# Two trunk layers in fp32: the first sum of weight blocks in the seven products, by an adding DMA load instead of VectorE

## The chip, the cores and the metric

The kernel runs on one core of a Trainium2 chip. The metric is the device time of one execution in microseconds (us). The engines are TensorE (PE, matmuls; PEld is its weight load), VectorE (DVE), ScalarE (ACT), GpSimd (POOL) and SyncE (SP), which here issues loads. Each engine works through its own list of instructions in order and waits on semaphores for others. DMA transfers are issued on an engine's queue and run on 16 DMA engines.

## The reference

Two layers run over 128 context tokens and 512 latent tokens, 640 in all, of width 1024. Each layer has two feed-forward parts (FFNs) with a mixer between them; the first layer's mixer is a convolution beside a gated recurrence, the second's is attention. All is float32. What the change touches is the first product of the four FFNs:

```python
def swiglu(h, w_in, w_out):
    gt, up = jnp.split(h @ w_in, 2, axis=-1)
    return (jax.nn.silu(gt) * up) @ w_out

def ffn_sublayer(x, mod, g, w_in, w_out, slot):
    h = pre_norm(x, g, mod[:, 3 * slot], mod[:, 3 * slot + 1])
    return x + 0.5 * mod[:, 3 * slot + 2] * swiglu(h, w_in, w_out)
```

`w_in` is 1024 x 5632 (2816 gate columns, then 2816 up columns), `w_out` 2816 x 1024.

## The kernel before

**Precision.** A float32 matmul is made of three matmuls of parts: each operand is split into a high part, rounded by a cast on ScalarE (line 609), and a low part, the rest, by a subtraction on VectorE (line 610). `split_x` makes both.

**The first product of an FFN.** The 2816 gate and up columns are cut into 22 blocks of 128 columns; block j has a gate block and an up block of 1024 x 128 each. The first two blocks are multiplied plainly (`plain_pair`). The other 20 go through `strassen`, a scheme with seven products in the place of eight: the weights are the 2 x 2 blocks a11, a12 (first and second half of the rows of the gate block), a21, a22 (of the up block), each 512 x 128; the tokens are halves of 320. Every product is 12 matmuls of 128 x 320 (four row tiles, three terms). Four products need sums of weight blocks, made on VectorE by `summed` (line 742):

```python
S1 = a21 + a22    # product 5
S2 = S1 - a11     # product 6
S3 = a11 - a21    # product 7
S4 = a12 - S2     # product 3
```

and products 1, 2 and 4 take a11, a12 and a22 as they are. The weights of product i of block j, cast and low part, lie in a tile `ws{i}_{j}`. Over four FFNs this makes 80 blocks and 80 sums of each kind. The results are put together by VectorE (lines 780, 784, 788) and ScalarE (lines 778, 786) and written as high and low parts of the hidden activations, `g{j}`.

**Order.** `ffn` writes a list of jobs (block, product). Within a block the order is 1, 5, 6, 2, 7, 3, 4; at the start of an FFN the first two blocks with seven products are mixed: (2,1), (2,2), (3,1), (3,2), then (2,5) and the rest. Blocks come in four parts of 6, 6, 6 and 4; after each part `project_out` multiplies by the rows of `w_out` (matmuls `po`, line 623) and frees `g`. Before the seven products the token sums are made by `norm_sums`: `t13_q` on VectorE (line 546), `t24_q` on GpSimd (lines 547, 548), and their high and low parts (`tchi`, `tclo`, `tdhi`, `tdlo`, two tiles of half the sum each).

**Loads.** `load_w` (line 567) loads a weight block on SyncE's queue into one of 4 `raw` buffers, at a raised priority (`AHEAD`, 400), so that a scheduler puts the load before other work of its time. A load whose buffer is not free stops SyncE's queue.

**Slots.** Sums and other passing tiles are put by `slot()` into 18 slots of 128 x 640 and into halves of pair tiles; `free()` gives them back, and a slot freed longest ago is taken first. A tile put in a used slot waits for the slot's last reader. S1 is freed after S2 is made, S2 and S4 after product 3's parts, S3 after product 7's. Some tiles print under an older name of their buffer (an S1 as `ma`, for one).

The names in the rows: `raw_wg`, `raw_wu` gate and up block, `S` any of the four sums, `ws` their parts, `pa`, `pb`, `pc` the PSUM banks of the products (product 5 opens `pc`), `st` results on their way, `po` the output projection.

Of the kernel before, what the change touches and what calls it, by code (L numbers as in the profile page):

```python
# [13 lines left out]
ALU = mybir.AluOpType  # L14
AX = mybir.AxisListType

P = 128
# [16 lines left out]
AHEAD = 400  # L34
# [41 lines left out]
def run(steps):  # L76
    for _ in steps:
        pass


class Trunk:
# [564 lines left out]
    def ffn(self, l, which, n, last):  # L646


        w_out = self.i["ffn_w_out"][l, which]
        pairs = {}  # L650
        mm = self.bank["mm"]
        ring = {"b": mm[0:3], "c": mm[3:5], "a": mm[5:6]}
        g = {}

        def bank(kind, name):
            ring[kind].append(ring[kind].pop(0))
            return self.psum.tile([P, 512], F32, tag=f"bank{ring[kind][-1]}", name=name)[:, 0:HW]

        def do(j, i):
            p = pairs.setdefault(j, dict(done=set()))  # L660
            for r, nm in enumerate(("gate", "up")):
                if nm not in p and (r == 0 or i not in (1, 2)):
                    p[nm] = self.load_w(*self.ffn_first(l, which, j)[r])
            self.strassen(p, j, i, bank, g)

        plain = EARLY if n == 0 else PLAIN
        order = [(j, c) for j in range(plain) for c in range(2)]
        if n:
            order.sort(key=lambda x: x[1])
        weights = {}  # L670
        for j, c in order:
            if j not in weights:
                weights[j] = [(self.weights(*x), x[1]) for x in self.ffn_first(l, which, j)]
            self.plain_pair(j, c, weights[j], g)
        self.free(*[f"b12_{q}" for q in range(4)])
        for q in range(4):
            self.norm_sums(q)
        jobs, ends = [], {}
        for part, (f0, fn) in enumerate(PARTS):
            js = list(range(f0, f0 + fn))  # L680
            if part == 0:
                js = js[plain:]
                first = js[:FIRST_TWO]
                jobs += [(j, i) for j in first for i in (1, 2)]
                jobs += [(first[0], i) for i in (5, 6, 3, 7)]
                for j, nxt in zip(first, first[1:]):
                    jobs += [(nxt, 5), (j, 4), (nxt, 6), (nxt, 3), (nxt, 7)]
                nxt = js[FIRST_TWO]
                jobs += [(nxt, 1), (first[-1], 4)] + [(nxt, i) for i in (5, 6, 2, 7, 3, 4)]
                js = js[FIRST_TWO + 1:]  # L690
            jobs += [(j, i) for j in js for i in (1, 5, 6, 2, 7, 3, 4)]
            ends[len(jobs)] = part
        self.points = self.points[plain:]
        for at, (j, i) in enumerate(jobs):
            do(j, i)
            if i == 4:
                self.point()
                if (l, which, j) in self.pieces:
                    self.mod_piece(*self.pieces.pop((l, which, j)))
                    if not self.pieces:  # L700
                        self.free("cond32")
            if at + 1 in ends:
                part = ends[at + 1]
                f0, fn = PARTS[part]
                if part == len(PARTS) - 1:
                    self.free_operand()
                js = range(f0, f0 + fn)
                run(self.project_out(w_out[f0 * P:(f0 + fn) * P, :], [g[j][0] for j in js], [g[j][1] for j in js], n,
                                     final=(part == len(PARTS) - 1), last=last))
                self.free(*[f"g{j}" for j in js])  # L710
        if not last:
            self.norm_chunk(n + 1, 1)
# [19 lines left out]
    def strassen(self, p, j, i, bank, g):  # L732


        nc = self.nc
        a11, a12 = p["gate"][:, 0:4], p["gate"][:, 4:8]
        if "up" in p:
            a21, a22 = p["up"][:, 0:4], p["up"][:, 4:8]

        def summed(name, x, y, op):  # L740
            t = self.slot(f"{name}_{j}", n=512).rearrange("p (k m) -> p k m", m=P)
            nc.vector.tensor_tensor(out=t, in0=x, in1=y, op=op)  # L742
            p[name] = t
            return t

        with self.tc.high_priority(offset=SPLIT_AHEAD):
            if i == 5:
                src = summed("S1", a21, a22, ALU.add)
            elif i == 6:
                src = summed("S2", p["S1"], a11, ALU.subtract)  # L750
            elif i == 7:
                src = summed("S3", a11, a21, ALU.subtract)
            elif i == 3:
                src = summed("S4", a12, p["S2"], ALU.subtract)
            else:
                src = a11 if i == 1 else a12 if i == 2 else a22
            w = self.wp.tile([P, KD * P], F32R, tag="w", name=f"ws{i}_{j}").rearrange("p (k m) -> p k m", m=P)
            self.split_x(src, w[:, 0:4], w[:, 4:8])
            if i == 6:
                self.free(f"S1_{j}")  # L760
            elif i == 7:
                self.free(f"S3_{j}")
            elif i == 3:
                self.free(f"S2_{j}", f"S4_{j}")
        kind = {1: "b", 6: "b", 7: "b", 4: "b", 5: "c", 3: "c", 2: "a"}[i]
        if i in (1, 5, 2):
            p[kind] = bank(kind, f"p{kind}")
        ps = p[kind]
        x = {1: "11", 2: "21", 3: "22", 4: "T4", 5: "T1", 6: "T2", 7: "T3"}[i]
        for k in range(4):  # L770
            xhi, xlo = self.B[x, k]
            for t, (a, b) in enumerate(((w[:, k], xhi), (w[:, k], xlo), (w[:, 4 + k], xhi))):
                nc.tensor.matmul(ps, lhsT=a, rhs=b, start=(i in (1, 5, 2) and k == 0 and t == 0),  # L773
                                 stop=(k == 3 and t == 2), skip_group_check=True)
        with self.tc.high_priority(offset=POST_AHEAD):
            if i in (1, 5, 6):
                p[i] = t = self.stp.tile([P, HW], F32, tag="st", name=f"st{i}")
                nc.scalar.copy(out=t, in_=ps)
            elif i == 4:
                nc.vector.tensor_tensor(out=p[1], in0=p[1], in1=ps, op=ALU.mult)  # L780
                self.hidden(g, j, 0, p[1])
            else:
                t = p[{2: 1, 7: 5, 3: 6}[i]]
                nc.vector.tensor_tensor(out=t, in0=t, in1=ps, op=ALU.add)  # L784
                if i != 7:
                    nc.scalar.activation(out=t, in_=t, func=AF.Silu)
                if i == 3 and 7 in p["done"] or i == 7 and 3 in p["done"]:
                    nc.vector.tensor_tensor(out=p[6], in0=p[6], in1=p[5], op=ALU.mult)
                    self.hidden(g, j, 1, p[6])
        p["done"].add(i)  # L790
# [856 lines left out]
```

## Time and profile before

| | |
|---|---|
| time, median of 3 runs | 2524.88 us (2524.49 to 2527.0) |
| the profiled execution's own time | 2523.16 us |
| its span, first to last instruction | 2521.4 us |
| TensorE busy | 2437.3 us, 97% |
| VectorE busy | 1982.7 us, 79% |
| ScalarE busy | 1122.1 us, 45% |
| GpSimd busy | 224.5 us, 9% |
| mean granted TensorE clock | 0.989 |

The shares are means over the whole span; they tell which engine has no room, not where. The list of waits tells for what TensorE stood. The timeline tells at a place when an operation ended that gives a buffer back, and when the work that needs the next content began; the difference is what a later content may take. An operation on VectorE is longer in its row than the distance to the next start, since operations follow each other with an overlap.

### The profile page before, as it was taken

To read this page: it belongs to the slowest core of one execution; us is meant where nothing else is said; L and a number is where in the kernel's file an instruction comes from. 1 tells how busy PE (TensorE), PEld (TensorE's weight loads), DVE (VectorE), ACT (ScalarE), POOL (GpSimd) and SP (SyncE) were. 2 spreads that over 40 slices of the span, in tenths; PEclk is the share of its full clock that TensorE was granted. 3 is DMA by queue.
4 is the path that set the end of the run, shared out by engine and by line. 5 is a ranking of instruction groups with operands and counts; after the bars stand their busy time and mean duration, and the time that the engine had idled before them with its cause. 6 is when DMAs were issued, how large, how long until landed. Compare 5 with 4: busy or idle time off the path is not lost. (4 is left out here: it accounts for less than half of the span.)

```text
span 2521.4 us, 43474 instructions
## 1 busy us (share of the span) xinstructions
PE 2437.3 (97%) x17072; PEld 2347.9 (93%) x17072; DVE 1982.7 (79%) x3750; ACT 1122.1 (45%) x2278; POOL 224.5 (9%) x308
## 2 busy tenths in 40 slices
PE   7999999999989999999999999999999999999999
PEld 5889999998989989999999899999988899999999
DVE  6889888868997678988887788888777868585755
ACT  6425243543234452525255343434556655252533
POOL 0000000104234110000011000000132111000000
PEclk8999999999999999999999999999999999999999
DMA  8453534412111226343440644344300121232322
GB/s 246 123 178 115 150 113 142 142 46 60 55 45 39 78 67 184 107 137 105 138 139 24 193 122 133 112 129 126 100 28 15 35 80 44 75 87 82 89 80 76
DMA packets 378261, 254.53 MB, mean 101 GB/s; under 512 B 9302, under 2 KB 362953, under 8 KB 378057
## 3 DMA queue, kind: packets, MB, share of 16 engines
q1 hardware_dynamic: 373112, 248.35, 33.7%
q10 hardware_dynamic: 4944, 3.41, 0.5%
q8 instruction: 134, 2.20, 0.4%
q14 instruction: 71, 0.57, 0.1%
HBM read 248.32 MB, written 3.41 MB: 100 GB/s over the span
## 5 line engine op out<-in xcount | busy, mean ns | idle before, releaser
L623 PE MATMUL po<-g,whi_o 128*128 128x256 f32 (+2 forms) x2672 | 579.0, 309 | 2.7 <-DVE st L780 1.1
L623 PEld LDWEIGHTS po<-g,whi_o 128*128 128x128 f32 x2672 | 442.8, 188 | 12.3 <-issue 2.9
L623 PE MATMUL po<-g,wlo_o 128*128 128x256 f32 (+2 forms) x1336 | 408.5, 307 | 0.2 <-DVE wlo_o L610 0.2
L814 DVE SCALAR_TENSOR_TENSOR x<-po,modG,x 128x256 f32<-128x256 f32 (+3 forms) x480 | 196.5, 435 | 127.1 <-PE po L623 125.5
L349 DVE SCALAR_TENSOR_TENSOR ma<-raw_wm,cond,ma 128x512 f32<-128x512 f32 x364 | 263.7, 753 | 33.2 <-DMA raw_wm<-in_w_mod 33.0
L609 ACT CAST ws<-S 128x512 fp32r<-128x512 f32 x290 | 180.3, 622 | 222.0 <-DVE S L742 72.9
L609 ACT CAST whi_o<-raw_o 128x768 fp32r<-128x768 f32 (+1 forms) x142 | 110.4, 777 | 351.9 <-PE po L623 220.7
L623 PEld LDWEIGHTS po<-g,wlo_o 128*128 128x128 f32 x1336 | 250.8, 188 | 0.4 <-DVE wlo_o L610 0.4
L773 PE MATMUL pb<-tdhi,ws 128*128 128x320 f32 x960 | 222.9, 312 | 5.8 <-DVE st L784 4.9
L610 DVE TENSOR_TENSOR ws<-S,ws 128x512 fp32r<-128x512 f32 x290 | 199.1, 688 | 31.5 <-ACT ws L609 30.7
L773 PE MATMUL pc<-b,ws 128*128 128x320 f32 x1140 | 191.2, 309 | 0.0
L773 PE MATMUL pb<-tdlo,ws 128*128 128x320 f32 x600 | 184.9, 309 | 0.0
L773 PEld LDWEIGHTS pb<-tdhi,ws 128*128 128x128 f32 x960 | 162.2, 188 | 13.3 <-DVE st L784 9.6
L773 PEld LDWEIGHTS pc<-b,ws 128*128 128x128 f32 x1140 | 173.4, 188 | 0.0
L405 POOL TENSOR_TENSOR acc<-acc,sq 128x320 f32<-128x320 f32 (+2 forms) x38 | 37.6, 991 | 1351.4 <-ACT sq L404 955.5
L610 DVE TENSOR_TENSOR wlo_o<-raw_o,whi_o 128x768 fp32r<-128x768 f32 (+1 forms) x142 | 126.4, 890 | 30.8 <-ACT whi_o L609 18.9
L773 PE MATMUL pb<-b,ws 128*128 128x320 f32 x700 | 145.7, 309 | 0.8 <-DVE x L814 0.8
L609 ACT CAST ws<-raw_wg 128x512 fp32r<-128x512 f32 x160 | 98.9, 620 | 81.6 <-PE po L623 32.3
L610 DVE TENSOR_TENSOR ws<-raw_wg,ws 128x512 fp32r<-128x512 f32 x160 | 109.8, 688 | 27.8 <-ACT ws L609 27.7
L976 DVE SCALAR_TENSOR_TENSOR cw<-pad,vecs,cw 128x655 f32<-128x655 f32 x120 | 121.5, 1014 | 1.8
L773 PE MATMUL pb<-tclo,ws 128*128 128x320 f32 x400 | 122.2, 308 | 0.0
L773 PE MATMUL pa<-bchi,ws 128*128 128x320 f32 x520 | 116.2, 310 | 6.0 <-DVE st L784 6.0
(509 smaller groups left out, 5742.8 us busy)
## 6 DMA issues: line engine op xcount, KB each, us to landing
raw_wm<-in_w_mod SPq DMA_DIRECT2D x144, 512.0 KB, 4.0
raw_wg<-in_ffn_w_in SPq DMA_DIRECT2D x88, 512.0 KB, 4.1
raw_wu<-in_ffn_w_in SPq DMA_DIRECT2D x88, 512.0 KB, 4.0
raw_o<-in_ffn_w_out SPq DMA_DIRECT2D x96, 384.0 KB, 3.5
raw_o<-in_ffn_w_out SPq DMA_DIRECT2D x32, 256.0 KB, 3.0
raw_z<-in_ev_w_in SPq DMA_DIRECT2D x8, 512.0 KB, 3.9
raw_oq<-in_od_w_in SPq DMA_DIRECT2D x8, 512.0 KB, 5.0
raw_o<-in_od_w_out SPq DMA_DIRECT2D x16, 256.0 KB, 3.0
```

The costliest lines, as they stand in the source:

```text
L349: nc.vector.scalar_tensor_tensor(out=acc, in0=part, scalar=col, in1=acc, op0=ALU.mult, op1=ALU.add)
L405: nc.gpsimd.tensor_tensor(out=self.acc[:, c0:c0 + n], in0=self.acc[:, c0:c0 + n], in1=sq[:, 0:n], op=ALU.add)
L609: nc.scalar.copy(out=hi, in_=src)
L610: nc.vector.tensor_tensor(out=lo, in0=src, in1=hi.bitcast(F32), op=ALU.subtract)
L623: self.last_mm = nc.tensor.matmul(ps, lhsT=a[k], rhs=b[k][:, c0:c0 + n], start=(k == 0 and j == 0), stop=(k == nk - 1 and j == 2))
L773: nc.tensor.matmul(ps, lhsT=a, rhs=b, start=(i in (1, 5, 2) and k == 0 and t == 0), stop=(k == 3 and t == 2), skip_group_check=True)
L814: nc.vector.scalar_tensor_tensor(out=xs, in0=ps[:, s0 - c0:s0 - c0 + sn], scalar=self.modG[:, n, m, g:g + 1], in1=xs, op0=ALU.mult, op1=AL ...
L976: nc.vector.scalar_tensor_tensor(out=y, in0=x[:, j:j + T + 15], scalar=col(j), in1=y, op0=ALU.mult, op1=ALU.add)
```

## The change

The sum S1 is no longer made by VectorE. When `do` loads the up block of a block with seven products, it also takes the slot of S1 there, loads the first half of the up block's rows (a21) into it on SyncE's queue, and then adds the second half (a22) to it by a DMA on GpSimd's queue with `accum_op=add`. Each of the two moves 512 rows of 512 bytes, 256 KB. Both are at the raised priority `AHEAD`. `strassen` takes that tile as product 5's source. The whole up block is still loaded into its raw buffer for S3 and products 7 and 4. So 80 additions leave VectorE, and 80 loads on SyncE and 80 adding loads on GpSimd, which issued no DMA before, are new.

```diff
--- before.py
+++ after.py
@@ -661,6 +661,13 @@
             for r, nm in enumerate(("gate", "up")):
                 if nm not in p and (r == 0 or i not in (1, 2)):
                     p[nm] = self.load_w(*self.ffn_first(l, which, j)[r])
+                    if r:
+                        with self.tc.high_priority(offset=AHEAD):
+                            p["S1"] = self.slot(f"S1_{j}", n=512).rearrange("p (k m) -> p k m", m=P)
+                            up = self.ffn_first(l, which, j)[1][0]
+                            self.nc.sync.dma_start(out=p["S1"], in_=up[0:4 * P].rearrange("(k p) m -> p k m", p=P))
+                            self.nc.gpsimd.dma_start(out=p["S1"], in_=up[4 * P:].rearrange("(k p) m -> p k m", p=P),
+                                                     accum_op=ALU.add)
             self.strassen(p, j, i, bank, g)
 
         plain = EARLY if n == 0 else PLAIN
@@ -745,7 +752,7 @@
 
         with self.tc.high_priority(offset=SPLIT_AHEAD):
             if i == 5:
-                src = summed("S1", a21, a22, ALU.add)
+                src = p["S1"]
             elif i == 6:
                 src = summed("S2", p["S1"], a11, ALU.subtract)
             elif i == 7:
```

Lines behind the inserted ones are numbered 7 higher in the changed kernel.

The first place is SyncE's queue at the second part of the second FFN (`01` in the names), before the change: gate and up blocks 6 to 8 and a piece of `w_mod` (`raw_wm`). Names end in a tile's number; `waits` lists whose semaphores a row waits for.

```order
L567 DMA raw_wg01_6_10459<-in_ffn_w_in 128x8x128 [waits DMAHW6_49,DVE_49]
L567 DMA raw_wu01_6_10479<-in_ffn_w_in 128x8x128 [waits DMAHW5_49,DVE_49]
L567 DMA raw_wm1_0_0_10600<-in_w_mod 128x1024 [waits DMAHW0_49,DVE_49]
L567 DMA raw_wg01_7_10606<-in_ffn_w_in 128x8x128 [waits DMAHW7_49,DVE_49]
L567 DMA raw_wu01_7_10626<-in_ffn_w_in 128x8x128 [waits DMAHW1_49,DVE_49,Activation_49]
L567 DMA raw_wg01_8_10741<-in_ffn_w_in 128x8x128 [waits DMAHW2_49,DVE_49]
L567 DMA raw_wu01_8_10761<-in_ffn_w_in 128x8x128 [waits DMAHW3_49,DVE_49]
```

The same place after the change; the rows of line 668 are the first halves of the S1 sums.

```order
L567 DMA raw_wg01_6_10483<-in_ffn_w_in 128x8x128 [waits DMAHW6_49,DVE_49]
L567 DMA raw_wu01_6_10503<-in_ffn_w_in 128x8x128 [waits DMAHW5_49,DVE_49]
L567 DMA raw_wm1_0_0_10625<-in_w_mod 128x1024 [waits DMAHW0_49,DVE_49]
L567 DMA raw_wg01_7_10631<-in_ffn_w_in 128x8x128 [waits DMAHW7_49,DVE_49]
L668 DMA S1_8_10789<-in_ffn_w_in 128x4x128 [waits PE_49]
L668 DMA S1_9_10931<-in_ffn_w_in 128x4x128 [waits PE_49]
L668 DMA S1_10_11067<-in_ffn_w_in 128x4x128 [waits PE_49]
L668 DMA S1_6_10505<-in_ffn_w_in 128x4x128 [waits PE_49,Pool_49]
L668 DMA S1_7_10653<-in_ffn_w_in 128x4x128 [waits DMAHW1_49,PE_49]
L567 DMA raw_wu01_7_10651<-in_ffn_w_in 128x8x128 [waits DMAHW2_49,DVE_49,Activation_49]
L567 DMA raw_wg01_8_10767<-in_ffn_w_in 128x8x128 [waits DMAHW3_49,DVE_49]
L567 DMA raw_wu01_8_10787<-in_ffn_w_in 128x8x128 [waits DMAHW4_49,DVE_49]
```

Five loads of S1 stand in a row behind gate block 7, in the order 8, 9, 10, 6, 7, and the up block of 7 and block 8 come behind them; GpSimd's adding loads stand in the same order. S1_8 to S1_10 wait for TensorE: for the last matmuls of the output projection on `g1`, `g3`, `g5`.

The second place is VectorE at the start of the seven products of the third FFN (`10` in the names), before the change, from the last reader of `t13_3` on.

```order
L610 TENSOR_TENSOR tclo3_14315<-t13_3_14310,tdlo2_14307 128x640
L742 TENSOR_TENSOR S1_2_14399<-raw_wu10_2_14397 128x512
L610 TENSOR_TENSOR tdlo3_14318<-t24_3_14311,tclo3_14315 128x640
L610 TENSOR_TENSOR ws5_2_14401<-S1_2_14399,ws5_2_14401 128x512
L784 TENSOR_TENSOR st1_14377<-st1_14377,pa_14382 128x320
L742 TENSOR_TENSOR S2_2_14419<-S1_2_14399,raw_wg10_2_14321 128x512
L742 TENSOR_TENSOR S4_2_14438<-raw_wg10_2_14321,S2_2_14419 128x512
L610 TENSOR_TENSOR ws6_2_14421<-S2_2_14419,ws6_2_14421 128x512
L742 TENSOR_TENSOR S3_2_14457<-raw_wg10_2_14321,raw_wu10_2_14397 128x512
L610 TENSOR_TENSOR ws3_2_14440<-S4_2_14438,ws3_2_14440 128x512
L742 TENSOR_TENSOR S1_3_14481<-raw_wu10_3_14479 128x512
```

The same place after the change.

```order
L610 TENSOR_TENSOR tclo3_14355<-t13_3_14350,tdlo2_14347 128x640
L610 TENSOR_TENSOR tdlo3_14358<-t24_3_14351,tclo3_14355 128x640
L791 TENSOR_TENSOR st1_14417<-st1_14417,pa_14422 128x320
L749 TENSOR_TENSOR S2_2_14460<-S1_2_14439,raw_wg10_2_14361 128x512
L610 TENSOR_TENSOR ws5_2_14442<-S1_2_14439,ws5_2_14442 128x512
L610 TENSOR_TENSOR ws6_2_14462<-S2_2_14460,ws6_2_14462 128x512
L749 TENSOR_TENSOR S4_2_14479<-raw_wg10_2_14361,S2_2_14460 128x512
L749 TENSOR_TENSOR S3_2_14498<-raw_wg10_2_14361,raw_wu10_2_14437 128x512
L610 TENSOR_TENSOR ws3_2_14481<-S4_2_14479,ws3_2_14481 128x512
L610 TENSOR_TENSOR ws7_2_14500<-S3_2_14498,ws7_2_14500 128x512
```

S1_2 and S1_3 (line 742) are gone, and S2 (now line 749) is the first sum of a block there; `st1` and the low part `ws6_2` moved ahead of a sum; the rest keeps its order.

The third place is SyncE after the change at the same start; before, these rows were there without those of line 668.

```order
L668 DMA S1_5_14869<-in_ffn_w_in 128x4x128 [waits DVE_49,Activation_49,Pool_49]
L668 DMA S1_2_14439<-in_ffn_w_in 128x4x128 [waits DVE_49,PE_49,Pool_49]
L567 DMA raw_wm1_2_0_0_14562<-in_w_mod 128x4x256 [waits DMAHW5_49,DVE_49]
L668 DMA S1_3_14522<-in_ffn_w_in 128x4x128 [waits DMASW1_49,DVE_49]
L567 DMA raw_wm1_2_0_1_14568<-in_w_mod 128x4x256 [waits DMAHW3_49,PE_49]
L567 DMA raw_wg10_4_14641<-in_ffn_w_in 128x8x128 [waits DMAHW7_49,DMAHW6_49,DVE_49]
L567 DMA raw_wm1_2_1_0_14680<-in_w_mod 128x4x256 [waits DVE_49]
L567 DMA raw_wm1_2_1_1_14686<-in_w_mod 128x4x256 [waits DMAHW5_49,DMAHW0_49,PE_49]
L668 DMA S1_4_14701<-in_ffn_w_in 128x4x128 [waits DMAHW1_49,DMASW2_49,DVE_49]
```

The load of S1_2 waits for VectorE (the `tclo3` row above), that of S1_3 for VectorE's low part of S4_2 (`ws3_2`), and pieces of `w_mod`, gate block 4 and up block 4 stand behind them.

## Rows read from the trace of the kernel before

**Rows 1.** The page's first part: busy time, share of the span, instructions of each engine.

```profile
PE 2437.3 (97%) x17072; PEld 2347.9 (93%) x17072; DVE 1982.7 (79%) x3750; ACT 1122.1 (45%) x2278; POOL 224.5 (9%) x308
```

**Rows 2.** List of TensorE's waits: us in total, times, longest.

```profile
PE pa L773 <- DVE st L784: 7.7, 4, 2.2
...
PE pb L773 <- DVE st L784: 4.9, 9, 1.6
...
PE pc L773 <- ACT ws L609: 4.1, 3, 1.6
```

**Rows 3.** Groups by form, VectorE: busy us, mean ns, idle before by releaser.

```profile
L742 DVE TENSOR_TENSOR S<-raw_wu 128x512 f32<-128x512 f32 x65 | 47.0, 723 | 24.2 <-DMA raw_wu<-in_ffn_w_in 23.3
```

**Rows 4.** DMA issues: count, KB each, median us from issue to landing.

```profile
raw_wu<-in_ffn_w_in SPq DMA_DIRECT2D x88, 512.0 KB, 4.0
...
raw_o<-in_ffn_w_out SPq DMA_DIRECT2D x32, 256.0 KB, 3.0
...
out_y_sample<-y ACTq DMA_DIRECT2D x8, 256.0 KB, 2.4
...
xr<-in_x_sample SPq DMA_DIRECT2D x4, 256.0 KB, 6.3
```

**Rows 5.** Timeline, VectorE and ScalarE, where t13_3 is read last: start, duration in us.

```profile
72.15 0.82 DVE L610 TENSOR_TENSOR tclo<-t,tchi 128x640 fp32r<-128x640 f32 x1
...
1373.38 0.90 DVE L610 TENSOR_TENSOR tclo<-t,tdlo 128x640 fp32r<-128x640 f32 x1 [0.40 <-ACT tdlo L609]
...
1374.38 1.19 DVE L742 TENSOR_TENSOR S<-raw_wu 128x512 f32<-128x512 f32 x1
...
1376.00 0.62 ACT L609 CAST ws<-S 128x512 fp32r<-128x512 f32 x1
...
2112.41 0.90 DVE L610 TENSOR_TENSOR tchi<-t,tchi 128x640 fp32r<-128x640 f32 x1 [0.39 <-ACT tchi L609]
```

**Rows 6.** Timeline, TensorE: first matmul of product 5, blocks 2 and 3.

```profile
78.73 0.31 PE L773 MATMUL pc<-tchi,ws 128*128 128x320 f32 x1
...
85.78 0.31 PE L773 MATMUL pc<-tchi,ws 128*128 128x320 f32 x1
...
1376.67 0.41 PE L773 MATMUL pc<-tchi,ws 128*128 128x320 f32 x1 [1.60 <-ACT ws L609]
...
1384.88 0.31 PE L773 MATMUL pc<-tchi,ws 128*128 128x320 f32 x1
...
2115.70 0.64 PE L773 MATMUL pc<-tchi,ws 128*128 128x320 f32 x1 [0.93 <-ACT ws L609]
...
2124.85 0.31 PE L773 MATMUL pc<-tchi,ws 128*128 128x320 f32 x1
```

**Rows 7.** Timeline, fourth FFN, block 8 to 9: VectorE and TensorE.

```profile
2227.51 0.69 DVE L742 TENSOR_TENSOR S<-raw_wg,S 128x512 f32<-128x512 f32 x1
...
2228.13 0.49 DVE L610 TENSOR_TENSOR g<-st,g 128x320 fp32r<-128x320 f32 x1
...
2228.53 0.48 DVE L780 TENSOR_TENSOR st<-st,pb 128x320 f32<-128x320 f32 x1
...
2241.43 0.31 PE L773 MATMUL pc<-tchi,ws 128*128 128x320 f32 x1
```

**Rows 8.** Timeline, TensorE: second FFN, first part's end, block 6.

```profile
1010.48 0.34 PE L623 MATMUL po<-g,wlo_o 128*128 128x384 f32 x1
...
1013.84 0.31 PE L773 MATMUL pc<-tchi,ws 128*128 128x320 f32 x1
```

**Rows 9.** Timeline, third FFN, blocks 13 to 15: VectorE and TensorE.

```profile
1608.03 0.69 DVE L610 TENSOR_TENSOR ws<-ma,ws 128x512 fp32r<-128x512 f32 x1
...
1620.03 0.31 PE L773 MATMUL pc<-tchi,ws 128*128 128x320 f32 x1
...
1632.35 0.31 PE L773 MATMUL pc<-tchi,ws 128*128 128x320 f32 x1
```

**Rows 10.** Windows: busy us of each engine, PEclk, DMA share, GB/s.

```profile
2110.00:2120.00 10.00, 7.01 (x27) 6.38 (x28) 8.61 (x12) 4.62 (x11) 2.20 (x2) 0.66 0.00 0
```

## The prediction

> **What bounds the kernel now.** I read the shares of busy time first: TensorE is busy 97% of the span, VectorE 79%, GpSimd 9% [rows 1]. So VectorE's work costs time only where TensorE waits for it. The list of what TensorE waits for gives, for the seven products, three entries that end in VectorE or in the casts that follow its sums: 7.7, 4.9 and 4.1 us, together 16.7 us in 16 waits [rows 2]. That is all that the removed work can give back. The removed work is in the table of groups by form: 65 of the 80 S1 sums took 723 ns each [rows 3] (the other 15 print under an older name of their buffer), 80 x 0.723 = 58 us. Third come the transfers, since the sum becomes one: 256 KB took 2.4 us from issue to landing at the least (a store of y), 3.0 for a weight tile and 6.3 at the most (loads of x); a 512 KB weight tile took 4.0 [rows 4], so a further 256 KB on SyncE's queue costs 1.0.
>
> Last I read, at the places where a block's first sum is made, when its slot becomes free and when product 5 needs it. That distance decides. In before S1 is written by one VectorE operation of 0.7 us behind the slot's last reader. Now, in the same slot, a load must pass SyncE's queue and land, and an adding load must follow and land. I write **A** for the second and take 3.0 us for the first [rows 4], so from the slot's release to a finished S1 it is L = 3.0 + A.
>
> **A itself** has no row: GpSimd issues no DMA in before. Bounds from the nearest rows: 2.4 and 6.3 us for 256 KB [rows 4]. I take 4.5, nearest to the 512 KB row's 4.0 and half a us above it, since an adding load reads the tile and the source and writes the tile; hence L = 7.5, ends 5.4 and 9.3. The Trainium skill (DMA: Bandwidth & Descriptors, section Anatomy of one DMA — SWDGE (gpsimd) path) has a fit for a copy issued on that queue, about 2 us plus the bytes over 436e3, by which 256 KB take an estimated 2.6 us; no run here shows one, and by it the time would be near rival 1 below.
>
> **VectorE's relief.** Of the 16 waits each can shrink by one S1 sum of 0.7 us at most, 11 us in all; I guess that half of them have such a sum ahead of what ends them: -5 (bounds 0 and -16.7). The rest of the 58 us lay under TensorE's work and gives nothing.
>
> **Starts of the four FFNs.** S1_2, the first to be made, takes the slot of t13_3, whose last reader is the operation that writes tclo3 (tchi3 in the fourth). It ends at 72.97, 1374.28 and 2113.31 us in the first, third and fourth FFN [rows 5]; the second reads like the third. Product 5 started at 78.73, 1376.67 and 2115.70 [rows 6]. Now it starts at release + 7.5 + 0.67, the last from the cast's start to its first matmul (1376.00 [rows 5] to 1376.67): 81.1, 1382.4 and 2121.5, later by 2.4, 5.8 (also in the second) and 5.8, in all **+19.8**. The next, S1_3, takes the slot of S4_2, which comes free six VectorE operations behind S1_2 (five spacings of 0.62 and 0.69 for the last [rows 7]: 3.8 us), so product 5 of block 3 follows that of block 2 by 3.8 + 7.5 = 11.3 us, where it was 7.05, 8.21 (twice) and 9.15 [rows 6]: 4.2 + 3.1 + 3.1 + 2.1 = **+12.5**. Block 4 comes 12 us or more later and isn't touched.
>
> **Second FFN, second part.** S1_8, S1_9 and S1_10 stand ahead of S1_6 on SyncE and on GpSimd, and wait for the last matmul of the output projection, which ends at 1010.8; product 5 of block 6 started at 1013.84 [rows 8]. Four loads on one queue land after 3.0 + 3 x 1.0 = 6.0 us, the add takes 4.5, the cast 0.67: 1022.0, **+8.2** (ends 6.1 and 10).
>
> **Third FFN, within a part.** S1_j takes the slot of S4_(j-1), free after the low part of product 3: block 13's ends at 1608.72 and product 5 of block 14 starts at 1620.03 [rows 9], 11.3 us later. Less 7.5 and 0.67 there are 3.1 to spare. But the chain closes on itself: S1, S2, S4, S3, casts and low parts, then again the slot. In between VectorE does eight operations of 128x512 and six of 128x320, spaced 0.62 and 0.40 [rows 7], together 7.4 us, so a block takes 7.5 + 7.4 = 14.9 where it took 12.3 (1620.03 to 1632.35 [rows 9]): 2.6 over in each. Runs of such blocks (8 to 11, 13 to 17, 19 to 21) lose 3 x 2.6 - 3.1, 4 x 2.6 - 3.1 and 2 x 2.6 - 3.1 = 4.7 + 7.3 + 2.1 = **+14**. Four of these loads stand on SyncE behind a gate block's load that waits for a low part two VectorE operations (some 1.4 us) later: **+6**.
>
> **Fourth FFN.** Here the slot is that of S2_(j-1), free when S4_(j-1) is made: 2228.20, needed at 2241.43 [rows 7], 13.2 us; less 8.2 there are 5 to spare. The loop is shorter, seven operations of 0.62 and four of 0.40 = 5.9: 5.9 + 7.5 - 12.3 = 1.1 over, 4 x 1.1 stays below 5: **0** (19 at A = 6.3). In the first FFN and the rest of the second most slots come free early: 0.
>
> **The clock.** TensorE stood before product 5 in the fourth FFN, and the granted clock was 0.66 in the mean of 2110 to 2120 [rows 10], with its matmuls at 0.64 us [rows 6], the 1.2 GHz level: 10 x 0.34 = 3.4 us lost. Of the like stalls in the second and third FFN neither did this (0.41 us in [rows 6]): one in three. The cases above make some 11 stalls of 2 us or more: 11 / 3 x 3.4 = **+12** (ends 4 and 20).
>
> **Sum**: -5 + 19.8 + 12.5 + 8.2 + 14 + 6 + 12 = +67.5, on the profiled execution's 2523.16 (1.8 above its span): 2590.7. The median of the runs, 2524.88, is 1.7 above that execution: **2592 us**.
>
> **Rivals.**
> 1. *The add is short* (A = 2.4). Starts: 0.3 + 3 x 3.7 = 11.4 and 2.1 + 1.0 + 1.0 = 4.1; second FFN 6.1; the loops of the third and fourth stay inside what there is to spare, 0; clock 4; relief -5: +21, **2546** (2534 with all 16.7 of the relief). For it: the 3.0 of a plain tile of that size. Against: twice the bytes moved in the tile.
> 2. *The add is long* (A = 6.3, as the loads of x). Starts 27 + 20, second FFN 10, third 35 + 6, fourth 19, clock 20, relief -5: +132, **2657**. For it: 512 short rows, and a queue that GpSimd serves. Against: no weight tile took 6.3.
> 3. *VectorE holds GpSimd back.* Beside a GpSimd operation the S1 sum took 1.19 us (at 1374.38 [rows 5]), where the mean is 0.72 [rows 3]: the two hinder each other, and an issue on GpSimd may wait for one VectorE operation, 0.7 us, in each add. Between forecast and rival 2 a us of A is worth (2657 - 2592) / 1.8 = 36 us, so 0.7 makes +25: **2617**. The Trainium skill (SBUF — State Buffer, section SBUF: two separate sides) has a rule that speaks against this change: descriptors of a DMA issued on GpSimd's queue are written by its cores, which are locked out while certain VectorE operations run; no run here shows a DMA on that queue, but the slower sum beside GpSimd agrees with a port that both use.
> 4. *The relief decides: faster.* If a finished S1 is there within 2 us of its slot's release, or the slots come free sooner than I read from the order, product 5 keeps its starts and only -5 to -16.7 is left: **2508 to 2520**. For it: TensorE does wait on VectorE at these places. Against: 3.0 us for the first of two transfers alone.
> 5. *Nothing measurable*: relief and late starts cancel. This needs a short add and all of the relief, and then still misses by 9.
>
> **Chances.** Forecast (A from 3.5 to 5.3) 0.45; short add 0.2; long add 0.15; GpSimd held back 0.1; faster 0.06; nothing 0.04. A measurement of this kernel tells about 0.2%, 5 us, from no change. So faster 0.06, same 0.04, slower 0.90. The range reaches from the short add with two thirds of the relief, 2538, to the long add, 2657; it leaves out rivals 4 and 5 and the tails of the first two.
>
> **What would show it.** In the profile after: 80 adding loads, some 4.5 us from issue to landing; TensorE waiting for ws of product 5 behind S1's DMA (a new entry in the list of waits, 40 to 60 us) at 74 to 90, 916 to 935, 1012 to 1022, 1375 to 1395 and 2114 to 2135, and in blocks 9 to 21 of the third FFN, 14 to 15 us apart and not 12.3; none in the fourth FFN's later blocks; more stretches at half clock. I am wrong if A is below 2.5 or above 6.5, if those starts do not move, or if a queue itself is the wait: SyncE held by a slot, with gate and up blocks late behind it.

## The result: slower by 8.4%

The changed kernel takes 2736.45 us in the median of 4 runs (2728.73 to 2747.78) where the kernel before took 2525.94 in the runs beside it: a ratio of 1.0841, with a 95% interval of 1.081 to 1.0872. Forecast were 2592 us and a range of 2538 to 2657. The direction was right, the size a third of what came: 67 us forecast, 210 measured. The profiled execution took 2728.73 us with a span of 2727.0 and a mean granted clock of 0.963; against the profiled execution of before that is 205.6 us more.

The page's first part (busy us, share, instructions) and two of its queues (packets, MB, share of 16 engines):

```profile
PE 2499.0 (92%) x17072; PEld 2398.6 (88%) x17072; DVE 1933.8 (71%) x3670; ACT 1116.1 (41%) x2278; POOL 326.8 (12%) x388
...
q1 hardware_dynamic: 415352, 269.33, 34.0%
...
q0 software_dynamic: 42240, 20.98, 6.3%
```

Against [rows 1] TensorE is busy 61.7 us longer with the same 17072 matmuls, which I put down to the clock (0.963 in the mean where it was 0.989), and so the other 144 us of the 205.6 are time in which it stands. VectorE lost 80 operations and 49 us. GpSimd's queue (q0) carries 42240 packets, 528 for each adding load, some 500 bytes each.

What TensorE waited for (us in total, times, longest), the lines that answer to [rows 2]:

```profile
PE pb L780 <- DVE st L791: 81.5, 37, 4.8
...
PE pc L780 <- ACT ws L609: 63.7, 16, 9.6
...
PE pa L780 <- DVE st L791: 9.1, 4, 3.2
```

The second, product 5's wait for the cast of S1, was 4.1 us and is 63.7, a little above the forecast's 40 to 60. The first was not forecast: product 4's or 6's wait for a read-out by VectorE, 4.9 us before.

DMA issues of the changed kernel, with the median time from issue to landing, which answer to [rows 4]:

```profile
raw_wg<-in_ffn_w_in SPq DMA_DIRECT2D x88, 512.0 KB, 4.4
...
S<-in_ffn_w_in SPq DMA_DIRECT2D x65, 256.0 KB, 3.5
...
S<-in_ffn_w_in POOLq DMA_DIRECT2D x65, 256.0 KB, 5.3
```

The adding load took 5.3 us where I had taken 4.5, the first load 3.5 and not 3.0, and a gate block on SyncE 4.4.

**A start, as forecast.** The timeline of the start of the fourth FFN (start and duration in us, engine, idle time before and what ended it):

```profile
2250.72 0.90 DVE L610 TENSOR_TENSOR tchi<-t,tchi 128x640 fp32r<-128x640 f32 x1 [0.40 <-ACT tchi L609]
...
2251.70 0.37 SPq L668 DMA_DIRECT2D S<-in_ffn_w_in  x1
...
2255.32 1.33 POOL L669 DMA_DIRECT2D S<-in_ffn_w_in  x1 [2.98 <-DMA S<-in_ffn_w_in]
...
2259.95 0.62 ACT L609 CAST ws<-S 128x512 fp32r<-128x512 f32 x1 [5.08 <-DMA S<-in_ffn_w_in]
...
2260.62 0.63 PE L780 MATMUL pc<-tchi,ws 128*128 128x320 f32 x1 [8.21 <-ACT ws L609]
```

VectorE's tchi3 ends at 2251.62, the slot's load is issued 0.1 us later, the adding load at 2255.32, and the cast of product 5 starts at 2259.95: L, from the slot's release to a finished S1, is 8.3 us. The cast to the first matmul takes 0.67, as I took it from [rows 5, 6]. TensorE stood for 8.21 us before that product.

**A block in the fourth FFN, not as forecast.** The timeline from S4 of block 8 to product 5 of block 9:

```profile
2391.19 0.68 DVE L749 TENSOR_TENSOR S<-raw_wg,S 128x512 f32<-128x512 f32 x1
...
2391.93 0.37 SPq L668 DMA_DIRECT2D S<-in_ffn_w_in  x1
...
2395.66 1.28 POOL L669 DMA_DIRECT2D S<-in_ffn_w_in  x1 [14.08 <-ACT st L785]
...
2400.78 0.62 ACT L609 CAST ws<-S 128x512 fp32r<-128x512 f32 x1 [5.14 <-DMA S<-in_ffn_w_in]
...
2400.80 0.69 DVE L749 TENSOR_TENSOR S<-S,raw_wg 128x512 f32<-128x512 f32 x1 [5.67 <-DMA S<-in_ffn_w_in]
...
2403.01 0.48 DVE L791 TENSOR_TENSOR st<-st,pb 128x320 f32<-128x320 f32 x1
...
2403.54 0.64 PE L780 MATMUL pb<-tdhi,ws 128*128 128x320 f32 x1 [3.08 <-DVE st L791]
...
2406.03 0.68 DVE L749 TENSOR_TENSOR S<-raw_wg,S 128x512 f32<-128x512 f32 x1
...
2408.64 0.31 PE L780 MATMUL pc<-tchi,ws 128*128 128x320 f32 x1
```

S4 ends at 2391.87 and gives back S2's slot; SyncE issues at 2391.93; GpSimd issues the adding load at 2395.66; the cast of S1 starts at 2400.78, so L is 8.9 us here. VectorE had nothing to do for 5.67 us, because S2, its next operation, waited for S1. Only behind S2 does it read out product 7 of block 8 (2403.01), and product 4 of block 8, which needs that bank, starts at 2403.54 after TensorE stood for 3.08 us. Product 5 of block 9 starts at 2408.64, 7 us after its cast: it waits for nothing. The next S4 starts at 2406.03, 14.84 us after the last, where a block took 12.3.

Windows over this stretch (length, busy us of each engine, granted clock, DMA share, GB/s):

```profile
2400.00:2404.00 4.00, 0.92 (x6) 0.65 (x5) 3.20 (x6) 2.12 (x4) 0.00 (x0) 0.93 0.01 1
...
2404.00:2408.00 4.00, 4.00 (x20) 4.00 (x20) 3.79 (x9) 2.43 (x5) 0.00 (x0) 0.65 0.02 4
...
2416.00:2420.00 4.00, 1.82 (x12) 1.56 (x12) 3.61 (x7) 2.74 (x5) 0.00 (x0) 1.00 0.00 0
...
2420.00:2424.00 4.00, 4.00 (x18) 4.00 (x18) 3.75 (x8) 1.91 (x4) 0.00 (x0) 0.57 0.02 7
...
2424.00:2428.00 4.00, 4.00 (x29) 4.00 (x28) 1.42 (x4) 1.89 (x4) 1.28 (x1) 1.00 0.58 165
```

TensorE stood for 3.1 us in the first of these windows and for 2.2 us in the one from 2416; in the 4 us behind them the clock stands at 0.65 and 0.57 of full, though TensorE is busy all of the time. Behind a stall of 1.8 us shortly before (2386.08 to 2387.87) it stayed at 1.00 from 2388 to 2392.

**Where the time went.** For each stage, how much later product 5 starts than in before at its end, less the same at its start (start times of the two traces; FFNs 1 to 4, product 5 of the blocks named; clock losses are in each stage):

| stage | forecast | changed | e1 | e2 | e3 | e5 |
|---|---|---|---|---|---|---|
| four starts, to block 3 | 32.3 | 36.8 | 5.9 | 34.0 | 2.5 | 12.1 |
| blocks 3 to 5, all FFNs | 0 | 17.1 | 10.5 | 16.0 | 11.0 | 1.7 |
| first FFN, from block 5 | 0 | 30.6 | 7.0 | 24.2 | 16.1 | 2.1 |
| second FFN, block 6 | 8.2 | 9.2 | 3.4 | 7.0 | 0.9 | 0.2 |
| second FFN, from block 6 | 0 | 15.8 | 6.0 | 11.9 | 14.9 | 4.7 |
| third FFN, from block 5 | 20 | 44.9 | 1.6 | 22.4 | 3.7 | 2.4 |
| fourth FFN, from block 5 | 0 | 50.9 | -0.5 | 38.9 | -1.0 | 0.5 |
| sum | 60.5 | 205.3 | 33.9 | 154.4 | 48.1 | 23.7 |

(The forecast had 12 us for the clock and -5 for VectorE's relief beside these; e1 to e5 are below.) Where I had counted a slot's release against product 5's need at a start, the sums hold within 5 us. They fail where I had written 0.

### The profile page after: what moved, and what is told of

It reads as the page before. It is cut to its first block, busy times and chain, and to the rows that moved or that the text cites. A ratio compares the mean times of both kernels' runs of the same rounds, so it can differ in the third digit from the quotient of the medians.

```text
span 2727.0 us, 43794 instructions
## 1 busy us (share of the span) xinstructions
PE 2499.0 (92%) x17072; PEld 2398.6 (88%) x17072; DVE 1933.8 (71%) x3670; ACT 1116.1 (41%) x2278; POOL 326.8 (12%) x388
## 3 DMA queue, kind: packets, MB, share of 16 engines
q0 software_dynamic: 42240, 20.98, 6.3%
## 5 line engine op out<-in xcount | busy, mean ns | idle before, releaser
L780 PE MATMUL pb<-tdhi,ws 128*128 128x320 f32 x960 | 244.5, 337 | 82.3 <-DVE st L791 81.5
L780 PEld LDWEIGHTS pb<-tdhi,ws 128*128 128x128 f32 x960 | 179.3, 207 | 95.0 <-DVE st L791 90.9
L669 POOL DMA_DIRECT2D S<-in_ffn_w_in x65 | 84.0, 1374 | 1155.1 <-DMA S<-in_ffn_w_in 440.3
L780 PE MATMUL pb<-tdlo,ws 128*128 128x320 f32 x600 | 194.5, 325 | 0.0
L780 PE MATMUL pc<-tchi,ws 128*128 128x320 f32 x460 | 127.0, 339 | 69.8 <-ACT ws L609 63.7
L749 DVE TENSOR_TENSOR S<-S,raw_wg 128x512 f32<-128x512 f32 x65 | 44.8, 690 | 166.1 <-DMA S<-in_ffn_w_in 143.1
L780 PEld LDWEIGHTS pc<-tchi,ws 128*128 128x128 f32 x460 | 86.5, 205 | 79.9 <-ACT ws L609 69.2
L780 PE MATMUL pb<-b,ws 128*128 128x320 f32 x700 | 152.9, 321 | 3.0 <-DVE x L821 3.0
```

The costliest lines, as they stand in the source:

```text
L669: self.nc.gpsimd.dma_start(out=p["S1"], in_=up[4 * P:].rearrange("(k p) m -> p k m", p=P), accum_op=ALU.add)
```

## The experiments

After the result there were three explanations. **Late slots**: S1 is made 8 to 9 us after its slot comes free, and that is the whole cost. **VectorE's order**: S2 stands in VectorE's queue ahead of read-outs of the block before, so that a late S1 holds these too. **Slow queues**: the new transfers delay gate, up and w_mod blocks on SyncE, or GpSimd's work hinders VectorE's. Some of the runs below have one execution only; four executions of the changed kernel lay within 19 us, so a difference of 10 us between such runs tells nothing.

### e1, e2: the price of the addition

```diff
-self.nc.gpsimd.dma_start(out=p["S1"], in_=up[4 * P:].rearrange("(k p) m -> p k m", p=P),
-                         accum_op=ALU.add)
+self.nc.gpsimd.dma_start(out=p["S1"], in_=up[4 * P:].rearrange("(k p) m -> p k m", p=P))
```

This is e2; e1 has only the first two lines of it.

> The adding load is left out, so S1 is a21 alone and a22 is missing from it (products 5, 6 and 3 are not the reference's). A finished S1 then needs some 3.5 us from its slot's release and no longer some 9. Late slots (S1 is made too late in a used slot): the wait list's entries for product 5 and product 4 (63.7 and 81.5 us) fall below 10 each, time 2525 to 2545. VectorE's order (S2 stands ahead of read-outs): the same, since S2's data is there in time. Slow queues (SyncE held by slot waits, gate and up blocks late behind it): those waits stay, 2570 or more.

> The second load is a plain copy on GpSimd's queue, with the same bytes, rows and waits, but without the addition, so S1 is a22 alone. If the addition in the DMA is what is slow, issue to landing falls from 5.3 us to about 3 and the time to 2590 to 2620. If the queue is, issue to landing stays near 5 and the time at 2715 to 2750. My guess is between: 4.5 us, 2690.

Measured: e1 2557.33 us (before beside it 2528.67), e2 2677.8 us. The waits of e1, then queue and issue of e2:

```profile
PE pc L778 <- ACT ws L609: 12.8, 5, 3.1
...
PE pb L778 <- DVE st L789: 11.2, 15, 1.5
```

```profile
q0 software_dynamic: 6400, 20.98, 2.8%
...
S<-in_ffn_w_in POOLq DMA_DIRECT2D x65, 256.0 KB, 4.0
```

A plain copy on GpSimd's queue landed 4.0 us after issue, in 80 packets of some 3.3 KB, where the adding load took 5.3 in 528. So of the 179 us between e1 and the changed kernel, the addition alone (1.3 us a load) is 59, and the second transfer in the path without any addition is 120. My guess of 4.5 us and 2690 lay near. e1 came 12 us above the range of late slots and below that of slow queues: even one load of 3.5 us costs 29 us, which is not in late starts (5.9 in the table) but in the blocks behind them and in the first two FFNs.

### e3, e5, e7: buffers of its own

```diff
-N_PAIRS, N_SLOTS, N_WIDE = 16, 18, 6
+N_PAIRS, N_SLOTS, N_WIDE = 16, 16, 6
...
+        self.s1p = pool("s1", 2)
...
-  p["S1"] = self.slot(f"S1_{j}", n=512).rearrange("p (k m) -> p k m", m=P)
+  p["S1"] = self.s1p.tile([P, 512], F32, tag="s1", name=f"S1_{j}").rearrange("p (k m) -> p k m", m=P)
...
```

This is e3, which also leaves out the `free` of S1; e5 is the same edit in the kernel before; e7 is e3 with `nc.gpsimd` in the place of `nc.sync` for the first load.

> S1 gets two buffers of its own (two of the 18 slots make room for them), so it waits for the readers of the S1 of two blocks before and no longer for a slot that comes free late; loads, addition and VectorE's work stay. Late slots: the waits before products 5 and 4 fall under 15 us in all and the time to 2515 to 2540. VectorE's order: the same, as S1 is there early. Slow queues, or GpSimd and VectorE hindering each other: 2570 or more.

> The kernel before (S1 by VectorE, no new loads) with the 16 slots and two S1 buffers of e3. If e3's remaining 44 us come from the two slots fewer, this takes 2560 to 2575; if they come from the 160 new transfers, 2520 to 2535.

> e3 with the first load also issued on GpSimd's queue, so that no S1 load stands on SyncE. If SyncE's order is the cost (S1 loads that wait hold gate, up and w_mod blocks behind them), 2515 to 2540, and VectorE's waits for raw_wg and raw_wu fall back to about those of before (10 and 32 us); if it is the transfers or GpSimd's work beside VectorE, 2560 or more.

Measured: e3 2569.98 us, ratio to before 1.0176 (1.0137 to 1.0215); e5 2546.46, 1.0059 (1.0041 to 1.0077); e7 2580.65, 1.0195 (1.0167 to 1.0222). e3 lies at the lower end of its range for slow queues, e5 between its two ranges, e7 in the one for transfers. In e3's list of waits the entry for product 5 and ScalarE's cast of S1 is gone and product 4's is

```profile
PE pb L779 <- DVE st L790: 19.5, 22, 3.0
```

and a gate block's issue to landing, before and in e3, is

```profile
raw_wg<-in_ffn_w_in SPq DMA_DIRECT2D x88, 512.0 KB, 4.1
...
raw_wg<-in_ffn_w_in SPq DMA_DIRECT2D x88, 512.0 KB, 5.0
```

With buffers of its own 167 us of the rise go, nearly all of the starts (2.5 left of 36.8) and of the loss of the third and fourth FFN (2.7 left of 95.8) among them: the late slot, with what follows from it, is what the change costs most. Of the remaining 44 us some 15 are the two slots fewer (e5), if the two costs add up; e5 loses 12.1 us at the starts, where e3 loses 2.5, so this split is rough. In the first two FFNs, where w_mod pieces are loaded too, e3 keeps about 25 us more than e5 (31.9 in the table less 7.0). It is not SyncE's order, since with all S1 loads on GpSimd (e7) it stays, gate blocks still land after 5.0 us, and VectorE's first sum of a block waits 38.5 us for gate blocks in all, where it was 41.9 in e3. In e3's trace the 7 gate blocks that had no other load in flight landed after 3.8 us (median; 3.9 for the 15 such blocks in before), the 43 with an S1 load in flight after 5.1 and the 26 with other loads only after 4.9. So a gate block is late where loads are in flight together; at what place they hold each other up is not shown.

### e6: the loads without a reader

```diff
-  p["S1"] = self.s1p.tile([P, 512], F32, tag="s1", name=f"S1_{j}").rearrange("p (k m) -> p k m", m=P)
+  p["S1d"] = self.s1p.tile([P, 512], F32, tag="s1", name=f"S1_{j}").rearrange("p (k m) -> p k m", m=P)
...
-                src = p["S1"]
+                src = summed("S1", a21, a22, ALU.add)
```

This is against e3; both loads fill `S1d`, which nothing reads.

> The kernel before with 16 slots, S1 by VectorE in a slot, and beside it the 160 new loads into two buffers that nothing reads. If the transfers themselves and their place in SyncE's and GpSimd's queues cost, 2555 to 2580 like e3; if what costs in e3 is only that S1 comes by them, 2520 to 2540.

Measured: 2676.37 us, ratio 1.0576 (1.0558 to 1.0594), above both ranges. The run doesn't answer its question. As nothing reads the loads, the scheduler put all 80 pairs into the first FFN, where SyncE stood for the adding load that had last filled the same buffer (us, times, longest; 60 to 620 us):

```profile
SPq L669 <- DMA S<-in_ffn_w_in: 306.7, 71, 8.2
```

Product 5 of the first FFN's last block came 141 us late, and the three other FFNs, with no such loads in them, added 12. It shows what a load that waits on SyncE's queue costs when others stand behind it.

### e4, e9, e10, e8: the order of the queues

e4 puts S2 behind the read-out of product 7 of the block before on VectorE, e9 also product 5's low part; e10 keeps the S1 loads in the order of the blocks on both queues; e8 issues both loads of the changed kernel on GpSimd's queue.

```diff
-                src = summed("S2", p["S1"], a11, ALU.subtract)
...
+                with self.tc.issue_after(self.st7):
+                    src = summed("S2", p["S1"], a11, ALU.subtract)
...
+                if i == 7:
+                    self.st7 = read.ins
```

This is e4, where `read` is the read-out of product 7.

> Only VectorE's order is changed: S2 of a block is put behind the read-out of product 7 of the block before (an edge of order, no wait on data). Loads and slots stay. VectorE's order: product 4's waits on that read-out (81.5 us) fall under 15, product 5's stay near 64, and the time falls by 50 to 90, to 2640 to 2685. Late slots alone (the loop from slot to slot sets the pace): the pace of some 15 us a block in the fourth FFN stays, the waits only move to product 5, and the time stays within 15 of 2736.

> As e4, and product 5's low part, the other VectorE operation that needs S1, is put behind the same read-out; in e4 it still stood ahead of it in every other block. If VectorE's order is what makes the fourth and third FFN lose where I saw time to spare, product 4's waits (81.5 us in the changed kernel, 37.4 in e4) fall under 15, and the time to 2650 to 2690. If the loop from slot to slot is, product 5's waits take their place (above 90) and the time stays at 2700 to 2725.

> The changed kernel with the S1 loads on SyncE and the adding loads on GpSimd in the order of the blocks, so that S1_14 of the first FFN no longer stands behind S1_16 and S1_6 of the second not behind S1_8 to S1_10. If the order of these queues cost the 6.5 us before product 5 of block 14 and the 9.8 before that of block 6, with the blocks behind, those two waits go and the time falls by 15 to 30, to 2705 to 2722; if S1 is late there by its slot alone, it stays within 10 of 2736.

> The changed kernel with late slots, both loads on GpSimd's queue. A finished S1 then needs about 4 + 5.5 us and GpSimd's two issues, some 10.5 us and not 9. Late slots: slower than 2736 by some 20 to 40. SyncE's order: faster, 2690 to 2715.

Measured: e4 2716.72, e9 2723.98, e10 2728.89, e8 2757.33 us. In e4 product 4's wait for the read-out fell from 81.5 to 37.4 us only, because product 5's low part now stood ahead of it in every other block, and product 5's rose to 74.0; the time, 20 us lower, lies between e4's two outcomes.

```profile
PE pc L783 <- ACT ws L609: 74.0, 23, 9.7
...
PE pb L783 <- DVE st L794: 37.4, 19, 4.6
```

The waits of e9:

```profile
PE pc L787 <- ACT ws L609: 88.9, 26, 9.5
...
PE pb L787 <- ACT st L792: 32.1, 30, 2.8
...
PE pb L787 <- DVE st L798: 4.4, 8, 1.1
```

In e9 product 4's wait for VectorE's read-out is down to 4.4 us, product 5's is 88.9 where it was 63.7, a wait for ScalarE's read-outs, which now stand behind its cast of S1, is 32.1 where it was 0.7, and the time fell by 12, little more than one execution can tell: the wait moved, as the second half of e9's expectation had it. So VectorE's order tells where the stall shows, and hardly how long it is. In the fourth FFN from block 5 e9 lost 38.3 us where the changed kernel lost 50.9; the starts took that back (51.7 us where it was 36.8). The order of the S1 loads (e10) is worth nothing that can be told, as its second outcome had it, though 14 of the first FFN does stand behind 16. e8 lost 21 us more, as late slots had it; its first load, on GpSimd's queue, took 4.0 us where SyncE's took 3.5. Freeing SyncE from S1 loads gave nothing.

### e11: S1 by GpSimd, without loads

```diff
-            nc.vector.tensor_tensor(out=t, in0=x, in1=y, op=op)
+            (nc.gpsimd if name == "S1" else nc.vector).tensor_tensor(out=t, in0=x, in1=y, op=op)
```

> The kernel before with the S1 sum made by a GpSimd operation in the place of VectorE's; no new loads. VectorE is relieved as in the change, and S1 comes about 1.5 to 2 us after its slot and raw block, not 9. Late slots: no new waits at the starts above 1 us each, 2515 to 2535. GpSimd beside VectorE: both slow down (1.2 us and not 0.7 in the trace of before), VectorE's busy time falls by less than 30 of the 58 us, and the time is 2535 to 2560.

Measured: 2568.84 us, ratio 1.0185 (1.0164 to 1.0207), above both ranges. The group of the sums on GpSimd and the page's first part:

```profile
L742 POOL TENSOR_TENSOR S<-raw_wu 128x512 f32<-128x512 f32 x65 | 90.8, 1396 | 1105.3 <-DMA raw_wu<-in_ffn_w_in 619.6 <-DVE S L742 138.8 <-PE mps L357 77.7
```

```profile
PE 2440.9 (95%) x17072; PEld 2348.6 (92%) x17072; DVE 1963.8 (77%) x3670; ACT 1118.2 (44%) x2278; POOL 338.6 (13%) x388
```

A sum took 1396 ns in the place of 723 [rows 3], and VectorE's busy time fell by 18.9 us, not 58: the other operations got longer beside GpSimd. TensorE is busy 4 us more and the rest of the 45 us is standing. So this run frees 18.9 us of VectorE and cannot tell what 58 would be worth. S1 also comes some 0.7 us and a handover later here; which part of the 45 us is that and which the slower VectorE is open.

### e12, e14, e13: an attempt to cut the loop

```diff
-                src = summed("S2", p["S1"], a11, ALU.subtract)
+                summed("S3", a11, a21, ALU.subtract)
+                src = summed("S2", a22, p["S3"], ALU.subtract)
...
+            if i == 5:      # product 5's low part
+                nc.gpsimd.tensor_tensor(out=w[:, 4:8], in0=src, in1=w[:, 0:4].bitcast(F32), op=ALU.subtract)
```

e12 frees S1's slot behind product 5, e14 behind product 6 as before; e13 has e3's buffers.

> The changed kernel with the loop cut: S2 is made as a22 - S3 (the same sum without S1), and product 5's low part by GpSimd, so no VectorE operation needs S1. In the fourth FFN S1 still takes the slot that the block before gives back after S4, with the same two loads; S4 no longer waits for an S1. If the loop from S1 over S4 to the next slot sets the pace, the fourth FFN goes back from some 15.5 to 12.3 us a block (no more than 5 us lost behind block 6, 50 in the changed kernel), product 4's waits (81.5 us) fall under 20 and the time to 2590 to 2650. If each S1 is late by itself, whatever the block before does, the fourth FFN still loses 30 or more and the time stays above 2690.

> e12 with S1's slot given back one step later, so that S2 no longer lands in the slot of its own block's S1 (in e12 it did, and the loop closed again through that slot, longer by GpSimd's low part). In the fourth FFN S1 then takes the slot of S3 of the block before, and the way from an S1 back to a later S1's slot goes over two blocks. If a loop within one block sets the pace, the fourth FFN loses under 12 us behind block 6 (50 in the changed kernel, 69 in e12), and the time comes to 2620 to 2690, with the starts of the four FFNs as late as before. If each S1 is late by itself, the fourth FFN still loses 30 or more and the time stays above 2700.

> e12's S2 and low part with e3's two S1 buffers: VectorE loses 160 operations (112 us) and waits for no S1 load. If what is left in e3 (44 us) is VectorE's queue behind late loads, 2530 to 2550; if it is the two slots fewer and the blocks that stand behind the S1 loads on SyncE, 2555 to 2580; if relief of VectorE is worth anything here, under 2525.

Measured: e12 2795.24, e14 2769.7 us, e13 2577.54 (ratio 1.0194, 1.0177 to 1.0211). VectorE's largest new wait in e12, with GpSimd's group of low parts there (busy us, mean ns), and in e14 the timeline of ScalarE and VectorE at a block of the fourth FFN:

```profile
DVE S L749 <- POOL ws L768: 151.5, 27, 10.9
...
L768 POOL TENSOR_TENSOR ws<-S,ws 128x512 fp32r<-128x512 f32 x65 | 87.3, 1342 | 575.7 <-ACT ws L767 575.7
```

```profile
2426.00 0.62 ACT L767 CAST ws<-S 128x512 fp32r<-128x512 f32 x1 [4.36 <-DMA S<-in_ffn_w_in]
...
2427.99 0.69 DVE L749 TENSOR_TENSOR S<-raw_wg,S 128x512 f32<-128x512 f32 x1 [6.88 <-POOL ws L768]
```

By the letter of the two expectations e12 and e14 gave the second outcome, each S1 late by itself. They don't decide it, since neither cut held. In e12 S2 takes the slot that S1 of its own block gives back, so VectorE waits for GpSimd's low part and the loop is closed again, longer by that operation (1.34 us): the fourth FFN from block 5 lost 71.2 us, or 4.5 a block over 16 blocks, where the changed kernel lost 3.2. In e14 ScalarE stands at the cast of S1 with casts of the same block behind it (4.36 us), S4 falls in S1's slot, and VectorE waits 6.88 us; 55.4 us lost. In both an engine that works in order still stood for the late S1 or its low part. e13 lies within 8 us of e3, in the second of its ranges: with S1 in time 80 further operations taken from VectorE gained nothing. VectorE's busy time fell by 14.0 us only (1937.9 to 1923.9), so that this too is a small relief.

## Why the forecast was wrong

**Right.** The loads stand in the way from a slot's release to product 5, and VectorE's shorter work (58 us removed, 49 less busy) is worth nothing against that. Step by step: the four starts 36.8 us (forecast 32.3), block 6 of the second FFN 9.2 (8.2), L 8.3 at a start (7.5). e3 shows that the slot is the cause: with early buffers the starts cost 2.5.

**A and L, mis-sized.** For A 4.5 was taken, 5.3 is the median from issue to landing; the first load took 3.5 and not 3.0; and L came to 8.3 at a start, 8.9 and 9.7 in two rounds of the fourth FFN. The rival "the add is long" (L = 9.3) came to 2657, still 79 us below what was measured: the size of L explains about 65 of the 144 us that the forecast missed, and the rest lies in steps that were put at nothing. e2 says the same: its second load took 4.0, less than the forecast's 4.5, L was 7.9 in a round shown below, and the time was 2677.8.

**The step that failed: "0" for the fourth FFN, and with it "to spare" in the third.** The prediction expected no waits in the fourth FFN's later blocks; it lost 50.9 us there. I had measured the time to spare from the slot's release to product 5 of the next block, 13.2 us [rows 7], less L. But the first operation that stands still for S1 is S2, on VectorE, and behind it in the same queue stands the read-out that product 4 of the block before needs. In before that product 4 starts here:

```profile
2237.91 0.31 PE L773 MATMUL pb<-tdhi,ws 128*128 128x320 f32 x1
```

That is 9.7 us behind the release at 2228.20, and from S2's start to that product pass 2.7 us (2400.80 to 2403.54), so 7.0 were left for L. With 8.9 nothing is to spare from the first block on, and then the loop counts in full: 14.84 us in the timeline, where the sum 5.9 + 7.5 gave 13.4 and took the difference out of 5 us that were not there. The next round of the changed kernel, and the round of e2 at the same block (S4, cast of S1, S4), show the loop again:

```profile
2416.38 0.63 ACT L609 CAST ws<-S 128x512 fp32r<-128x512 f32 x1 [3.59 <-DMA S<-in_ffn_w_in]
...
2421.67 0.68 DVE L749 TENSOR_TENSOR S<-raw_wg,S 128x512 f32<-128x512 f32 x1
```

```profile
2350.95 0.68 DVE L748 TENSOR_TENSOR S<-raw_wg,S 128x512 f32<-128x512 f32 x1
...
2359.56 0.62 ACT L609 CAST ws<-S 128x512 fp32r<-128x512 f32 x1 [4.15 <-DMA S<-in_ffn_w_in]
...
2364.82 0.68 DVE L748 TENSOR_TENSOR S<-raw_wg,S 128x512 f32<-128x512 f32 x1
```

L was 8.9, 9.7 and 7.9 us and the rounds took 14.84, 15.64 and 13.87: each is L and 5.9 to 6.0, the prediction's own 5.9. So the loop was right and the time to spare was wrong. By the prediction's rule with 8.9 (2.5 over in each of four blocks, less 3.6 to spare) a part would lose some 6 us, the three parts behind block 5 together 19; without anything to spare 16 blocks at 2.5 to 3.3 lose 40 to 53, and 50.9 were measured.

The loss in the fourth FFN over the runs goes with the length of the way: none with 3.5 us (e1), 2.4 us a block with 3.5 + 4.0 and GpSimd's handover (e2), 3.2 with 3.5 + 5.3 (the changed kernel; 3.3 in e10), 4.5 in e12, which has GpSimd's 1.34 us more in it and other changes too. Order alone (e4, e9) gave back at most 13 of the 50.9, since ScalarE's cast of S1 holds its own queue too. A kernel in which the loop is cut and the slot stays late was not reached, so that the loop rests on these rounds and runs; that the late slot is the cause rests on e3.

**"Block 4 isn't touched" failed too.** S1_4 takes S4_3's slot, and the chain that I stopped at block 3 goes on; blocks 4 and 5 lost 17.1 us. Only about 6 of these go with early buffers: 11.0 stay in e3 (1.7 in e5), so that most of them come with the loads and not with that chain. And **"in the first FFN and the rest of the second most slots come free early: 0"** hid 46.4 us. Late slots are only part of that: 31.0 of it stay with e3's own buffers and 6.8 with e5's, so about 24 come with the loads themselves.

**The clock was sized at 12 us by three stalls of before; it came to 62**, TensorE's longer busy time. The rule of one in three was read wrongly. Of the three waits before product 5 two were of 1.6 us and left the clock alone; the third, of 0.93 us, was not what lowered it, since it had fallen by then:

```profile
2110.00:2112.00 2.00, 0.00 (x0) 0.00 (x0) 1.95 (x3) 0.70 (x3) 0.24 (x1) 1.00 0.00 0
...
2112.00:2114.00 2.00, 1.93 (x10) 1.93 (x11) 1.51 (x3) 0.75 (x2) 1.92 (x2) 0.79 0.00 0
...
2114.00:2116.00 2.00, 1.07 (x4) 0.67 (x4) 1.74 (x3) 1.57 (x3) 0.04 (x1) 0.50 0.00 0
```

TensorE had stood all of 2110 to 2112. The new stalls are more and mostly longer, and behind the two shown above, of 3.1 and 2.2 us, the clock was low. (One sum of the prediction is off without bearing on this: the short add with two thirds of the relief gives 2540 and not the 2538 that the range starts at.)

The rival that VectorE holds GpSimd back is not shown: an issue of the adding load took GpSimd 1.28 us in the median and the load landed some 4 us after that. One issue in ten took 1.75 us or more, the longest 2.23, but the second longest (2.14 us, at 1076.07) had no VectorE operation beside it. The Trainium skill (DMA: Bandwidth & Descriptors, section Anatomy of one DMA — SWDGE (gpsimd) path) gives an estimated 2.6 us for a copy of 256 KB on this queue; e2 measured 4.0 for it from issue to landing, and the measurement decides.

No version here beats the kernel before; e5, which has no loads, is nearest and 0.6% slower.

## What to carry to other kernels

Before an operation on an engine is replaced by transfers, take the time from its buffer's release to the first need at every place, and count the need from the first operation that stands behind the waiting one in any engine's queue, not from the consumer that one has in mind. If the new content's readers lead back to the release of its next buffer, the longer way is paid in every round, and time to spare pays once at most. A buffer that is free a round earlier was worth 167 us here (e3); no run shows a gain from the work saved.

## What was unexpected of the hardware

The adding DMA moved its 256 KB in 528 packets where the plain copy of the same rows took 80, and landed in 5.3 us where the copy took 4.0. GpSimd was busy 1.28 us with an issue of the adding load in the median and 0.75 us with one of the copy. Eighty sums taken from VectorE and given to GpSimd shortened VectorE's busy time by 18.9 us only, of 58.
